# Seven-product pairs for six tiles of the attention branch's projection, in a one-core hybrid layer

## The chip, the core and the metric

The kernel runs on one core of a Trainium2 chip. The metric is the device time of one execution in microseconds (us). The kernel before took 874.84 us, the median of three runs (873.97 to 877.55). The profile shows one further execution.

## The reference, cut to what matters

One layer works on 640 token columns (128 of a prompt, 512 of a sample) and 1024 channels. It has two branches, a gated long convolution ("hyena", `y_h`) and an attention (`y_a`). What the change touches is the end, where both are merged:

```python
mod = silu(cond) @ w_ada + b_ada            # shift, scale, gate
p_h = (y_h * silu(g_h)) @ w_bh
p_a = (y_a * silu(g_a)) @ w_ba
m_h, m_a = split(sigmoid(m), 2, axis=-1)
out = (m_h * p_h + m_a * p_a) @ w_out
x_new = layer_norm(ALPHA * x + gate * out)
```

All tensors are float32.

## The kernel before

**Numbers.** A float32 operand is split into a high part (float32r, made by ScalarE, "ACT") and a low part (the rest, a subtraction on VectorE, "DVE"); see `split`, L100 to L102. A product takes three TensorE ("PE") matmuls: high x high, high x low, low x high. Channels lie on the partitions, tokens along the free axis. A row of 640 tokens is worked on in two halves of 320 columns, one PSUM bank each. All weights are 128 x 1024 tiles of one array `wall`; tiles 80 to 87 (`T_BH`) are `w_bh`, 88 to 95 (`T_BA`) `w_ba`, 96 on (`T_WO`) `w_out`.

**Plain tiles.** `proj` (L175) makes one output tile of 128 channels: 8 blocks of the contraction x 3 passes x 2 halves = 48 matmuls of 320 columns, at L170. Its weight comes through `wraw` (L133, a load into a ring of two raw tiles) and `wtile` (split into a "wh" ring of two and a "wl" ring of three).

**Pairs.** The projections of attention already go another way. `pair_tile` (L1174) makes two output tiles together: with contraction and outputs halved it is a 2 x 2 block product, which it forms from seven products instead of eight (the Winograd form of Strassen's method). The weights' side is prepared by `prepare` (L1142): four sums (L1154) of 512-column blocks, seven operands "wb", each split. The input's side, four sums `t1` to `t4` of the rows and their splits, is made once by `first_sums` and what follows it. A product is 4 blocks x 3 passes = 12 matmuls of 320 columns, at L1189; a pair is 84. Results are put together by ACT and DVE (L1196, L1198, L1204) and handed to a function `use`. After the fourth product the next pair of the list `follow` is prepared.

**Stages.** After the convolution come attention with its projections (from about 388 us; 19 pairs, woven with scores, softmax and values), then the merge in two halves, then the output projection with the norm (L1454, L1469 to L1480). The merge:

- the hyena half: eight plain tiles of `w_bh` on `yhH`, `yhL`. The first two are interleaved by half. Weight `T_BH + 2` is split into a place of its own (L1390). The result is multiplied by the gate row `mh` (L574), a row of the attention branch is loaded and split into `yaH`, `yaL` (L1396 to L1398), and a step of the generator `gate_rows` (L1338) is taken;
- the attention half: eight plain tiles of `w_ba` on `yaH`, `yaL`, multiplied by the gate row `ma`, added to `mh` on DVE (L1427), split into `mH`, `mL`;
- `gate_rows` forms the residual's gate on all partitions: eight loads of 512 KB (`wgate`), two DVE operations of 1024 columns for each (L1346, L1348). `gate_bias` (L1404) sums them over the partitions with 12 short matmuls (L1417) and adds the bias, after tile 4 of the attention half;
- `out_weight` loads and splits the eight tiles of `w_out`, four of them during the attention half.

**Order.** PE's order is the program's in most of the kernel. DVE's and ACT's orders are chosen by the scheduler from data that should be ready, except in instructions that are pinned. In the merge, loads (all issued on SP's queue, L63) keep the program's order; a load whose place isn't free yet holds those behind it. GpSimd ("POOL") carries the softmax's scaling (L1010), and issues the accumulating weight loads of the convolution (L150). The output's constants and residual rows (`bc`, `res`, L1482 to L1487) are loaded once the merge's tiles are released.

Of the kernel before, what the change touches and what calls it, by code (L numbers as in the profile page):

```python
# [9 lines left out]
F32 = mybir.dt.float32  # L10
# [35 lines left out]
def tile_hyena_natten_step(ctx: ExitStack, tc: tile.TileContext, a, o):  # L46
# [211 lines left out]
    def prologue():  # L258
# [19 lines left out]
        def begin(i):  # L278
            if i == 1:
                parts[i] = [[row(yhp, "yh", f"w1{t}{c}", dt)[:, :512] for c in range(2)] for t, dt in (("r", F32), ("h", F32R), ("l", F32R))]  # L280
            else:
                parts[i] = [
                    [t[:, 512 * c : 512 * c + 512] for c in range(2)] for t in (
                        wp.tile([P, 1024], F32, tag="raw", name=f"raw{i}"), wp.tile([P, 1024], F32R, tag="wh", name=f"wh{i}"),
                        wp.tile([P, 1024], F32R, tag="wl", bufs=3, name=f"wl{i}"),
                    )
                ]
            early[i] = [[parts[i][t][k // 4][:, P * (k % 4) : P * (k % 4) + P] for k in range(NK)] for t in (1, 2)]
# [853 lines left out]
    def prepare(i0, i1, pin):  # L1142
        for i in (i0, i1):
            if i not in raws:
                wraw(i)
                loads[i] = last[0]
        ra, rb = raws.pop(i0), raws.pop(i1)
        a11, a12, a21, a22 = (r[:, 512 * h : 512 * h + 512] for r in (ra, rb) for h in range(2))
        src = {0: a11, 4: a12, 5: a22}
        wb = {}  # L1150

        def wsum(j, x, y, op, dst=None):
            src[j] = dst if dst is not None else row(sp, "s", f"s{j}_{i0}", bufs=2)[:, :512]
            ins = nc.vector.tensor_tensor(src[j], x, y, op=op)  # L1154
# [19 lines left out]
    def pair_tile(i0, i1, use):  # L1174
        def halfrow(tag, bufs, name):
            return sp.tile([P, 384], F32, tag=tag, bufs=bufs, name=f"{name}{i0}")[:, :HALF]

        if i0 not in ready:
            prepare(i0, i1, False)
# [2 lines left out]
        for j in range(7):  # L1182
# [18 lines left out]
            else:  # L1201
                if j != 3:
                    c = halfrow("c", 4, f"c{j}_")
                nc.vector.tensor_tensor(c, dst, c if j == 3 else u, op=ALU.add)  # L1204
# [41 lines left out]
    def mix_(m):  # L1246
# [13 lines left out]
    out["slots_r"] = left.enter_context(tc.tile_pool(name="slots_r", bufs=1))  # L1260

    def yh_home(i):
        if i < 4:
# [5 lines left out]
    def yh_raw(n):  # L1269
# [2 lines left out]
                out["stage"] = slot(0, "v", f"yhraw{n}")  # L1272
            yraw[n] = out["stage"][:, NT * (n % 2) : NT * (n % 2) + NT]
        else:
            yraw[n] = slot(1, ("q", "ql")[n % 2], f"yhraw{n}")[:]
        load_to(yraw[n], yh_d[n])
        if n == 2:
            behind(last[0], loads[mix_(6)[1]])
# [34 lines left out]

    with tc.manual_schedule(engines={mybir.EngineType.PE}):
        values_back(1)
        for j in range(8):
            main, n_main = mains(j)
            if j in (3, 5):
# [8 lines left out]
    for n in range(2, NK):  # L1327
        yh_split(n)
        if n in (3, 4):
            yh_raw(n + 3)  # L1330
    mp = tail.enter_context(tc.tile_pool(name="mp", bufs=1, side="right"))
    lp = left.enter_context(tc.tile_pool(name="lp", bufs=1))
# [3 lines left out]
    gbc = lp.tile([P, 2, D], F32, tag="gbc", name="gbc")  # L1336

    def gate_rows():  # L1338
        for k in range(NK):
            raw = slot(k % 2, "v", f"gate{k}")[:, :D]  # L1340
            load_to(raw, a["wgate"][k])
            yield
            for c in range(2):
                s_ = st[:, k, c : c + 1]
                if k == 0:
                    ins = nc.vector.tensor_scalar_mul(gbc[:, c], raw, s_)  # L1346
                else:
                    ins = nc.vector.scalar_tensor_tensor(gbc[:, c], raw, s_, gbc[:, c], op0=ALU.mult, op1=ALU.add)  # L1348
                tc.keep_in_program_order(ins)

    wo = {}

    def wo_row(t, i, n):
        return lp.tile([P, D], F32R, tag=f"{t}{i}", name=f"{t}{i}_{n}")[:]

    def out_weight(k):
        raw = wp.tile([P, D], F32, tag="raw", name=f"wo{k}")
        load_to(raw[:], a["wall"][T_WO + k])
        if k < 4:
            wh, wl = (wo_row(t, k, T_WO + k) for t in ("woh", "wol"))  # L1360
        else:
            if k < 6:
                wh = slot(k - 4, "v", f"woh{k}", F32R)[:, :D]
            else:
                wh = wp.tile([P, D], F32R, tag="wh", name=f"woh{k}")[:]
            if k == 5:
                wl = wp.tile([P, D], F32R, tag="raw", name="wol5")[:]
# [5 lines left out]
    def mixed(src, n, tag, bufs):  # L1373
        th = row(mp, tag, f"{tag}{n}", bufs=bufs)
        load_to(th[:], src[n])
        return th

    side = gate_rows()
    mhs = []
# [6 lines left out]
    for n in range(NK):  # L1386
        if n < 2:
            ps = firsts[n]
        else:
            ps = now(proj(T_BH + n, yhH, yhL, dst=[[wo_row(t, 0, T_BH + n)] for t in ("woh", "wol")] if n == 2 else None))  # L1390
        wraw(T_BH + n + 2)
        th = mixed(mh_d, n, "mh", NK)
        mhs.append(th)
        for p, cs in zip(ps, CS):
            gate(th[:, cs], p)
        raw = slot(1, ("q", "ql")[n % 2], f"yaraw{n}")  # L1396
        load_to(raw[:], ya_d[n])
        split(yaH[n], yaL[n], raw[:])  # L1398
        next(side, None)
    mH, mL = yhH, yhL  # L1400
    eps = lp.tile([P, 1], F32, tag="eps", name="eps")
    nc.gpsimd.memset(eps[:], LN_EPS)

    def gate_bias():  # L1404
        quarter = lp.tile([P, 1], F32R, tag="quarter", name="quarter")
        nc.scalar.activation(quarter[:], eps[:], AF.Copy, scale=0.0, bias=0.25)
        b0 = wp.tile([P, D], F32, tag="raw", name="b0")
        load_to(b0[:], a["rows"][0:1].to_broadcast([P, D]))
        for c in range(2):
            for c0, n in ((0, 384), (384, 384), (768, 256)):  # L1410
                cs = slice(c0, c0 + n)
                gt = out["slots_r"].tile([P, 2, 384], F32R, tag="kl" if (c0 // 384 + c) % 2 else "k", name="gt")
                gh, gl = gt[:, 0, :n], gt[:, 1, :n]
                split(gh, gl, gbc[:, c, cs])
                pg = aux(f"gb{c}{c0}")
                for i, g in enumerate((gh, gl)):
                    nc.tensor.matmul(pg[:, :n], quarter[:].to_broadcast([P, P]), g, start=i == 0, stop=i == 1)  # L1417
                nc.vector.scalar_tensor_tensor(gbc[:, c, cs], b0[:, cs], 0.25, pg[:, :n], op0=ALU.mult, op1=ALU.add)

    for n in range(NK):  # L1420
        ps = now(proj(T_BA + n, yaH, yaL))
        if n < NK - 2:
            wraw(T_BA + n + 2)
        th = mixed(ma_d, n, "ma", 3)
        for p, cs in zip(ps, CS):
            gate(th[:, cs], p)
        nc.vector.tensor_tensor(th[:], th[:], mhs[n][:], op=ALU.add)  # L1427
        split(mH[n], mL[n], th[:])
        next(side, None)
        if 0 < n < 5:  # L1430
            out_weight(n - 1)
        if n == 4:
            gate_bias()

    for k in (4, 6, 7, 5):
        out_weight(k)


    tail.close()
# [190 lines left out]
```

## Time and profile before

| | |
|---|---|
| median of three runs | 874.84 us |
| the profiled execution | 874.77 us |
| its span | 873.0 us |
| TensorE matmul, busy | 861.0 us, 99% |
| VectorE, busy | 645.6 us, 74% |
| ScalarE, busy | 447.1 us, 51% |
| GpSimd, busy | 130.0 us, 15% |
| granted TensorE clock, mean | 0.997 |

The profile has a page (busy shares, 40 slices, the chain of work that ended last, the costliest groups) and views that are asked for: busy time by stage, groups of instructions, the chain and the instructions in order of time, waits. PEld is the loading of the matmuls' weights, which overlaps PE. A row of the timeline gives start, length, engine, line, operation, output <- inputs, shapes, how many; in brackets the idle time before it and who ended it. A row of a group gives the busy time of all, the mean length of one in ns, and the idle time ahead of them. Records on an engine overlap a little at their ends, so an engine's rate is read from the distance of starts.

### The profile page before, as it was taken

How to read it: one execution, taken by the hardware profiler on the slowest of the kernel's cores; microseconds unless marked ns; L12 is line 12 of the kernel's file. 1: busy time of each engine (PE TensorE's matmuls, PEld its weight loads, DVE VectorE, ACT ScalarE, POOL GpSimd, SP SyncE). 2: the span in 40 equal slices, each digit the busy share in tenths (PEclk: the TensorE clock that was granted, in tenths of full speed). 3: DMA queues.
4: the chain of work that ended last, by engine and by line, in shares of the span. 5: the costliest groups of instructions: out<-in, count | busy, mean ns of one | idle time of the engine just before them, and what ended most of it. 6: DMA issues, size and time to landing. Idle time of an engine off the chain costs nothing.

```text
span 873.0 us, 16814 instructions
## 1 busy us (share of the span) xinstructions
PE 861.0 (99%) x6446; PEld 833.0 (95%) x6446; DVE 645.6 (74%) x1310; ACT 447.1 (51%) x952; POOL 130.0 (15%) x143
## 2 busy tenths in 40 slices
PE   8999999999999999999999999999999999999996
PEld 7799999999999999999999999999999999999885
DVE  5685587769559747888977887877878567676656
ACT  4485655545553553646664666655656532233200
POOL 0211010101001010106221243222223100000000
PEclk9999999999999999999999999999999999999998
DMA  8977565566556567764162533533352588545511
GB/s 312 411 180 158 128 140 129 134 142 143 124 136 146 115 177 161 189 182 169 59 190 70 170 115 133 166 113 127 100 173 80 153 296 268 176 160 182 215 68 53
DMA packets 58308, 138.39 MB, mean 159 GB/s; under 512 B 8655, under 2 KB 25171, under 8 KB 58228
## 3 DMA queue, kind: packets, MB, share of 16 engines
q1 hardware_dynamic: 47140, 111.69, 38.5%
q0 software_dynamic: 5472, 19.93, 14.0%
q10 hardware_dynamic: 5616, 5.70, 1.9%
q8 instruction: 51, 0.84, 0.4%
q14 instruction: 29, 0.24, 0.1%
HBM read 121.17 MB, written 16.12 MB: 157 GB/s over the span
## 4 chain that ended last, share of the span: by engine, by line
PE 95%; DMA 2%; ACT 2%; DVE 1%; issue 0%; POOL 0%; DVEq 0%; ACTq 0%; POOLq 0%
PE mm L170 36%; PE sp L1189 27%; PE out L1454 6%; PE v L926 5%; PE pt L1028 3%; PE s L1035 3%; PE s L988 2%; PE mm L184 2%; DMA ada<-wada 2%; PE ve L938 1%; DMA wl<-wall 1%; PE adaT L253 1%; PE adaT L270 1%; PE yb L159 1%; PE yb L158 1%; PE yb L160 1%
## 5 line engine op out<-in xcount | busy, mean ns | idle before, releaser
L1189 PE MATMUL sp<-t,wb 128*128 128x320 f32 x912 | 142.0, 310 | 0.0
L1189 PEld LDWEIGHTS sp<-t,wb 128*128 128x128 f32 x912 | 135.2, 188 | 0.9 <-issue 0.7
L170 PE MATMUL mm<-hH,wh 128*128 128x320 f32 x480 | 112.8, 313 | 0.3 <-ACT hH L370 0.3
L170 PE MATMUL mm<-hL,wh 128*128 128x320 f32 x480 | 112.7, 310 | 0.0
L170 PE MATMUL mm<-hH,wl 128*128 128x320 f32 x480 | 112.6, 310 | 0.1
L1189 PE MATMUL sp<-hH,wb 128*128 128x320 f32 x456 | 111.2, 314 | 0.0
L170 PEld LDWEIGHTS mm<-hH,wh 128*128 128x128 f32 x480 | 80.1, 188 | 2.5 <-issue 1.4
L170 PEld LDWEIGHTS mm<-hL,wh 128*128 128x128 f32 x480 | 80.8, 188 | 0.9 <-DVE hL L378 0.4
L170 PEld LDWEIGHTS mm<-hH,wl 128*128 128x128 f32 x480 | 80.8, 188 | 0.8 <-DMA wl<-wall 0.3
L1189 PEld LDWEIGHTS sp<-hH,wb 128*128 128x128 f32 x456 | 78.5, 188 | 2.3 <-issue 2.1
L151 ACT ACTIVATE wh<-raw 128x1024 fp32r<-128x1024 f32 x38 | 40.4, 1062 | 73.4 <-PE mm L170 65.5
L150 POOL DMA_DIRECT2D wl<-wall x38 | 33.0, 868 | 299.5 <-ACT wl L149 238.8
L1189 PE MATMUL sp<-hL,wb 128*128 128x320 f32 x228 | 70.4, 309 | 0.0
L101 ACT ACTIVATE wb<-s 128x512 fp32r<-128x512 f32 x76 | 46.4, 629 | 31.0 <-DVE s L1154 24.2
L1010 POOL TENSOR_SCALAR p<-p,sm 128x384 f32<-128x384 f32 x32 | 44.3, 1393 | 103.7 <-DVE sm L1009 103.7
L102 DVE TENSOR_TENSOR wb<-s,wb 128x512 fp32r<-128x512 f32 x76 | 51.9, 697 | 7.9 <-ACT wb L101 7.7
L101 ACT ACTIVATE wb<-raw 128x512 fp32r<-128x512 f32 x57 | 35.8, 629 | 40.0 <-PE sp L1189 20.8
L102 DVE TENSOR_TENSOR wb<-raw,wb 128x512 fp32r<-128x512 f32 x57 | 40.6, 712 | 8.6 <-ACT wb L101 8.6
L1454 PE MATMUL out<-woh,yhs 128*128 128x512 f32 (+1 forms) x176 | 45.5, 372 | 0.0
L1189 PEld LDWEIGHTS sp<-hL,wb 128*128 128x128 f32 x228 | 42.9, 188 | 0.0
L170 PE MATMUL mm<-yhs,wh 128*128 128x320 f32 x224 | 41.9, 309 | 0.0
L149 ACT ACTIVATE wl<-raw 128x1024 fp32r<-128x1024 f32 x38 | 40.8, 1075 | 0.0
(377 smaller groups left out, 2038.5 us busy)
## 6 DMA issues: line engine op xcount, KB each, us to landing
raw<-wall SPq DMA_DIRECT2D x93, 512.0 KB, 3.7
wl<-wall POOLq DMA_DIRECT2D x38, 512.0 KB, 5.8
ada<-wada SPq DMA_DIRECT2D x16, 512.0 KB, 5.6
tm<-bias SPq DMA_DIRECT2D x16, 512.0 KB, 4.4
gate<-wgate SPq DMA_DIRECT2D x8, 512.0 KB, 4.3
wo<-wall SPq DMA_DIRECT2D x8, 512.0 KB, 4.1
xt<-xT SPq DMA_DIRECT2D x8, 320.0 KB, 7.3
dec<-decay SPq DMA_DIRECT2D x20, 128.0 KB, 3.3
```

The costliest lines, as they stand in the source:

```text
L101: hi = nc.scalar.activation(dst_h, src, AF.Copy)
L102: return hi, (eng or nc.vector).tensor_tensor(dst_l, src, f(dst_h), op=ALU.subtract)
L149: nc.scalar.activation(wl, raw[:], AF.Copy, scale=-1.0)
L150: nc.gpsimd.dma_start(wl, a["wall"][i], accum_op=ALU.add)
L151: nc.scalar.activation(wh, raw[:], AF.Copy)
L170: nc.tensor.matmul(ps[hf][:, :HALF], wt[k], x[:, hf * HALF : (hf + 1) * HALF], start=(i == 0 and k == 0), stop=(i == lead[2] and k == NK - ...
L926: nc.tensor.matmul(ps[t // 2][:, t % 2 * 256 : t % 2 * 256 + 256], x[:, k, P * t : P * t + P], wk, start=first and t % 2 == 0, stop=last, ...
L1010: nc.gpsimd.tensor_scalar_mul(pv, pv, sm[:, 2:3])
L1028: nc.tensor.transpose(pt[:, i * P : i * P + P], x, ident)
L1035: nc.tensor.matmul(dst, lhs, rhs, start=start, stop=stop, skip_group_check=True)
L1189: nc.tensor.matmul(dst, wk, x(xi, k), start=j < 4 and k == 0 and i == 0, stop=k == 3 and i == 2, skip_group_check=True,)
L1454: ins = nc.tensor.matmul(dst, m[k][:, c0 : c0 + P], w[:, c : c + n], start=(first and k == 0), stop=(last and k == 5), skip_group_check=True,)
```

## The change

- Tiles 0 to 5 of the attention half go through `pair_tile` as three pairs; tiles 6 and 7 stay plain.
- The four sums of the attention branch's rows are made in the hyena half (`turned_sums`), as rows land; rows are loaded in the order 0, 4, 1, 5, 2, 6, 3, 7.
- The addition of both branches moves from DVE to POOL, by half-rows, and trails a pair behind (`finish`).
- The gate rows move into attention: one DVE operation behind the fourth product of 16 of the 19 pairs, with one raw tile for the loads. `gate_bias` moves behind the first output tile, with 8 matmuls of 512 columns, and its bias row is loaded behind the residual rows.
- Weights of the hyena half are split two tiles ahead, and the third one loses its own place.
- The raw weight ring has three tiles; the rings `s` and `c` of the pairs are cut to size.
- The descriptor ring of DMAs issued by POOL shrinks from its default to 2048 bytes a partition, which frees SBUF.

```diff
-        raws[i] = wp.tile([P, 1024], F32, tag="raw", name=f"raw{i}")
+        raws[i] = wp.tile([P, 1024], F32, tag="raw", bufs=3, name=f"raw{i}")
...
+            if j == 3 and i0 in GATED_AT:
+                gate_row(after)
+                gate_load()
             if j == 3 and (i0, i1) in follow:
                 prepare(*follow[i0, i1], True)
...
+    GATED_AT = [runs[0][i][0] for i in (0, 1, 2, 3, 5, 6, 7, 8, 10, 11, 12, 13, 15, 16, 17, 18)]
...
+    def gate_row(after):
+        k, c = divmod(gate_n[0], 2)
+        s_ = st[:, k, c : c + 1]
+        if k == 0:
+            ins = nc.vector.tensor_scalar_mul(gbc[:, c], gate_raw[k], s_)
+        else:
+            ins = nc.vector.scalar_tensor_tensor(gbc[:, c], gate_raw[k], s_, gbc[:, c], op0=ALU.mult, op1=ALU.add)
+        behind(ins, after)
+        tc.keep_in_program_order(ins)
+        gate_n[0] += 1
...
+    def turned_sums(k):
+        b11, b12 = (ya_raw[k][:, cs] for cs in CS)
+        b21, b22 = (ya_raw[k + 4][:, cs] for cs in CS)
+        prev = {}
+        for t, x, y, op in (
+            ("t1", b12, b11, ALU.subtract), ("t3", b22, b12, ALU.subtract),
+            ("t2", "t1", b22, ALU.subtract), ("t4", "t2", b21, ALU.add),
+        ):
+            d = prev[t] = sp.tile([P, HALF], F32, tag="c", bufs=4, name=f"y{t}_{k}")[:]
+            nc.vector.tensor_tensor(d, prev.get(x) if type(x) is str else x, y, op=op)
+            split(ts[t][0][:, k], ts[t][1][:, k], d)
...
+        for n in range(NK):
+            ps = firsts[n] if n < 2 else now(proj(T_BH + n, yhH, yhL))
+            wraw(T_BH + n + 2)
...
+            load_to(mh(n), mh_d[n])
+            for p, cs in zip(ps, CS):
+                gate(mh(n)[:, cs], p)
+            if n < NK - 2:
+                early[T_BH + n + 2] = wtile(T_BH + n + 2)
+            ya_row(YA[n])
...
+        def merged(n, hf, src):
+            th = mas[n][:, CS[hf]]
+            gate(th, src)
+            pending.append((n, hf, th))
...
+        def finish():
+            if not pending:
+                return
+            n, hf, th = pending.pop(0)
+            nc.gpsimd.tensor_tensor(th, th, mh(n)[:, CS[hf]], op=ALU.add)
+            split(mH[n][:, CS[hf]], mL[n][:, CS[hf]], th)
...
+        for p, (i0, i1) in enumerate(pairs):
+            for i in (1, 0):
+                ma(2 * p + i)
+            for i, _ in enumerate(pair_tile(i0, i1, lambda i, hf, src: merged(2 * p + i, hf, src), ya_operand)):
+                if i in (1, 3, 5, 7):
+                    finish()
+                if p == 2 and i == 4:
+                    wraw(T_BA + 6)
+                    wraw(T_BA + 7)
+        for n in (6, 7):
+            ps = now(proj(T_BA + n, yaH, yaL))
+            ma(n)
+            for hf in range(2):
+                merged(n, hf, ps[hf][:, :HALF])
+            while pending:
+                finish()
+            for k in (0, 1) if n == 6 else (2, 3):
+                out_weight(k)
+        for k in (4, 6, 7, 5):
+            out_weight(k)
...
         ps = out_tile(t, ((0, 512), (512, 256), (768, 256)) if t == 4 else ())
+        if t == 0:
+            gate_bias()
         norm_tile(t, ps, t == 4)
...
-    nc = _bacc.Bacc("TRN2", target_bir_lowering=False, num_devices=1)
+    nc = _bacc.Bacc("TRN2", target_bir_lowering=False, num_devices=1, dynamic_dma_scratch_size=2048)
```

More of the change, by code (lines that the diff above doesn't have):

```diff
@@ L1203, in pair_tile @@
                     c = halfrow("c", 4, f"c{j}_")
-                nc.vector.tensor_tensor(c, dst, c if j == 3 else u, op=ALU.add)
+                after = nc.vector.tensor_tensor(c, dst, c if j == 3 else u, op=ALU.add)
                 if j != 2:
@@ L1315, in tile_hyena_natten_step @@
         values_back(1)
+        before = last[0]
+        gate_load()
+        behind(last[0], before)
         for j in range(8):
@@ L1366, in out_weight @@
             if k == 5:
[L1367 removed]
+                wl = wp.tile([P, D], F32R, tag="raw", bufs=3, name="wol5")[:]
             else:
@@ L1385, in tile_hyena_natten_step @@
         firsts = [now(gen) for gen in firsts]
[L1386 to L1436, printed above, removed]
+        for n in range(NK):
+            ps = firsts[n] if n < 2 else now(proj(T_BH + n, yhH, yhL))
+            wraw(T_BH + n + 2)
+            if n % 2 == 0:
+                mhp.append(mp.tile([P, 2 * NT], F32, tag=f"mh{n}", name=f"mh{n}"))
+            load_to(mh(n), mh_d[n])
[4 more added lines that the diff above has]
+            ya_row(YA[n])
@@ new lines, in gate_bias @@
+        def gate_bias():
+            quarter = lp.tile([P, 1], F32R, tag="quarter", name="quarter")
+            nc.scalar.activation(quarter[:], eps[:], AF.Copy, scale=0.0, bias=0.25)
+            b0 = gp.tile([P, D], F32, tag="gr", name="b0")
+            load_to(b0[:], a["rows"][0:1].to_broadcast([P, D]))
+            for c in range(2):
+                for half in range(2):
+                    cs = slice(512 * half, 512 * half + 512)
+                    g2 = fin.tile([P, D], F32R, tag="r", bufs=2, name="gt")
+                    gh, gl = g2[:, :512], g2[:, 512:]
+                    split(gh, gl, gbc[:, c, cs])
+                    pg = aux(f"gb{c}{half}")
+                    for i, g in enumerate((gh, gl)):
+                        nc.tensor.matmul(pg[:], quarter[:].to_broadcast([P, P]), g, start=i == 0, stop=i == 1)
+                    nc.vector.scalar_tensor_tensor(gbc[:, c, cs], b0[:, cs], 0.25, pg[:], op0=ALU.mult, op1=ALU.add)
@@ new lines, in tile_hyena_natten_step @@
+        pairs = [(T_BA + 2 * p, T_BA + 2 * p + 1) for p in range(3)]
+        for x, y in zip(pairs, pairs[1:]):
+            follow[x] = y
+        for p, (i0, i1) in enumerate(pairs):
[7 more added lines that the diff above has]
+                    wraw(T_BA + 7)
```

82 lines of the change are left out of this document (51 added, 31 removed).

## The prediction, made before the result was known

> **What bounds the kernel now.** I read the page first (busy shares, slices, chain), then busy time by stage, then the chain in order of time.
>
> ```profile
> span 873.0 us, 16814 instructions
> PE 861.0 (99%) x6446; PEld 833.0 (95%) x6446; DVE 645.6 (74%) x1310; ACT 447.1 (51%) x952; POOL 130.0 (15%) x143
> ...
> PEclk9999999999999999999999999999999999999998
> ...
> PE 95%; DMA 2%; ACT 2%; DVE 1%; issue 0%; POOL 0%; DVEq 0%; ACTq 0%; POOLq 0%
> ```
>
> TensorE is busy for 99% of the span at full clock and is 95% of the chain that ended last. A busy row need not be a dense one, so the second view takes stages: attention (four rows), the hyena half of the merge, its attention half.
>
> ```profile
> 388.00:436.00 48.00, 48.00 (x367) 46.35 (x367) 43.41 (x119) 32.92 (x92) 19.68 (x16) 1.00 0.37 120
> 436.00:532.00 96.00, 96.00 (x771) 93.27 (x770) 76.80 (x207) 59.01 (x152) 26.16 (x24) 1.00 0.43 139
> 532.00:612.00 80.00, 80.00 (x641) 77.64 (x639) 63.60 (x172) 48.70 (x127) 22.03 (x20) 1.00 0.40 129
> 612.00:695.00 83.00, 83.00 (x693) 79.92 (x692) 63.38 (x165) 52.25 (x129) 23.09 (x21) 1.00 0.41 124
> 695.00:752.00 57.00, 57.00 (x391) 57.00 (x390) 41.38 (x51) 17.80 (x23) 0.00 (x0) 1.00 0.81 275
> 752.00:810.00 58.00, 58.00 (x395) 57.92 (x395) 39.08 (x55) 20.14 (x26) 0.00 (x0) 1.00 0.46 158
> ```
>
> The columns are PE, PEld, DVE, ACT, POOL, then clock and DMA. PE fills every stage. In the merge DVE works 41.38 of 57 us and 39.08 of 58, and POOL nothing. The chain's longest pieces give the price of a matmul:
>
> ```profile
> 406.11 12.32 PE sp L1189 x84
> ...
> 695.21 91.52 PE mm L170 x624
> ...
> 809.70 55.39 PE out L1454 x264
> ```
>
> 91.52 us over 624 matmuls is 146.7 ns for each 320 columns, and 12.32 over 84 is 146.7 as well: a seven-product pair's matmuls run as densely as plain ones, once their operands are there. The merge ends at 809.70, when the output projection starts. The kernel is bound by the number of matmul columns; everything else has to stay out of their way.
>
> **The change, part by part.** *Products.* Six tiles of 48 matmuls (288) become three pairs of 7 x 12 = 84 (252). 36 x 146.7 ns = 5.28 us go from the only path that counts. This is the whole gain; the rest is cost, hidden or not.
>
> *Weights and results of the pairs*, on DVE. The timeline of DVE in attention has operations of both sizes, first with POOL at rest, then (the last two) with POOL at work:
>
> ```profile
> 469.09 0.68 DVE L102 TENSOR_TENSOR wb<-raw,wb 128x512 fp32r<-128x512 f32 x1
> 469.69 0.68 DVE L102 TENSOR_TENSOR wb<-s,wb 128x512 fp32r<-128x512 f32 x1
> 470.30 0.48 DVE L866 SCALAR_TENSOR_TENSOR ql<-c,q 128x320 fp32r<-128x320 f32 x1
> ...
> 498.26 0.48 DVE L574 SCALAR_TENSOR_TENSOR sg<-sg,c 128x320 f32<-128x320 f32 x1
> 498.66 0.68 DVE L1154 TENSOR_TENSOR s<-raw 128x512 f32<-128x512 f32 x1
> ...
> 504.06 0.83 DVE L102 TENSOR_TENSOR wb<-raw,wb 128x512 fp32r<-128x512 f32 x1 [0.35 <-ACT wb L101]
> ...
> 506.09 0.97 DVE L102 TENSOR_TENSOR wb<-s,wb 128x512 fp32r<-128x512 f32 x1
> ```
>
> Starts follow each other after 0.60 us for 512 columns (469.09 to 469.69) and after 0.40 for 320 (498.26 to 498.66). A pair issues 4 weight sums and 7 low parts of 512 columns, and of 320: 5 combinations of products, 4 gates and 4 low parts of the merged half-rows. That is 11 x 0.60 + 13 x 0.40 = 11.8 us of DVE in 84 x 146.7 ns = 12.3 us of PE. It fits, at 96%, where attention runs at about 80%. What makes it hold: five of the seven weights of the first pair are prepared in the hyena half; the last pair prepares none after it; a pair's weights are begun after product 4 of the pair before, so three products (3 x 12 x 146.7 ns = 5.3 us) lie between; and the low parts of merged rows may lag, since only the output projection reads them. I take 0 here, and keep 0 to 3 us of stall for the range. ACT stands at 20.14 of 58 us and has room.
>
> *Sums of the attention branch* (turned sums): 4 sets of 4 sums and 4 low parts of 320 columns, 32 x 0.40 = 12.8 us of DVE in the hyena half, with five weights and two sums of the first pair (about 5 us). The gate rows leave this place:
>
> ```profile
> L1348 DVE SCALAR_TENSOR_TENSOR gbc<-gate,st,gbc 128x1024 f32<-128x1024 f32 x14 | 17.3, 1278 | 0.0
> ...
> L1417 PE MATMUL gb<-gt,quarter 128*128 128x384 f32 (+1 forms) x12 | 3.3, 318 | 0.0
> ```
>
> Most of their 17.3 us was in the 57 us of that row, so DVE stays near 41 to 43 of 57. Cost 0 on the path, as long as the last set of sums comes ahead of the first pair. The gate rows' 8 loads of 512 KB leave the one stage whose DMA share is 0.81, which helps the rows of the attention branch to land.
>
> *Third weight of the hyena half.* It loses its own place, so its split waits until the first tile's matmuls are done. PE does 12 half-steps of 6 matmuls first: 695.21 + 72 x 0.1467 = 705.8, and needs it after 24 more, at 709.3.
>
> ```profile
> 696.79 1.22 DVE L102 TENSOR_TENSOR wol<-raw,woh 128x1024 fp32r<-128x1024 f32 x1
> ...
> 705.66 0.89 DVE L574 SCALAR_TENSOR_TENSOR mh<-mh,mm 128x320 f32<-128x320 f32 x2 [2.65 <-PE mm L170]
> 706.47 0.82 DVE L102 TENSOR_TENSOR ya_hL<-yaraw,ya_hH 128x640 fp32r<-128x640 f32 x1
> ```
>
> Now the split is over at 698.0; then its high part on ACT and 1.22 us on DVE fall between 705.8 and about 708.1, with the gates and one row's split (705.66 to 707.3) as company. About 1 us is spare. I take 0, bounds 0 to 2.
>
> *Gate rows in attention.* 14 x 1.28 us and two shorter ones, about 19 us of DVE, into stages with 4.6 + 19.2 + 16.4 + 19.6 = 59.8 us of DVE idle (the first four window rows). Behind each row on DVE stand the next pair's sums; PE needs them three products later.
>
> ```profile
> DVE c L1204 <- PE sp L1189: 27.9, 32, 2.4
> ...
> DVE s L1154 <- DMA raw<-wall: 5.7, 5, 2.4
> ```
>
> DVE is ahead there: its longest total wait, 27.9 us, is for PE. Only 388 to 436 is tight (90%), with three rows (3.8 us) for 4.6 us of idle time. SP gets 8 loads more, each queued behind a row on DVE through the single raw tile, and the weights are queued behind them. The third raw tile lets one weight load go ahead of that and can shorten the 5.7 us that DVE waits for them; off the path, 0. I take 0 for the move, bounds 0 to 4.
>
> *Addition on GpSimd.* The merge's sum of both branches goes from DVE to POOL, 12 + 4 half-rows of 320 columns.
>
> ```profile
> L304 POOL TENSOR_TENSOR wl<-raw,wh 128x512 fp32r<-128x512 f32 x1 | 1.4, 1383 | 8.3 <-DMA xt<-xT 8.3
> ...
> L304 POOL TENSOR_TENSOR w1l<-w1r,w1h 128x256 fp32r<-128x256 f32 x1 | 1.0, 976 | 0.0
> ```
>
> Between 0.98 (256) and 1.38 us (512), so about 1.1 each, 4.4 us of POOL in a pair. POOL is not idle company for DVE, though:
>
> ```profile
> 503.82 2.14 POOL L1010 TENSOR_SCALAR edge<-edge,sm 128x320 f32<-128x320 f32 x2
> 505.94 2.46 POOL L1010 TENSOR_SCALAR p<-p,sm 128x384 f32<-128x384 f32 x2
> ```
>
> Beside these the low parts at 504.06 and 506.09 take 0.83 and 0.97 us, against 0.68 alone: up to 0.3 us for each POOL instruction, 1.2 us for a pair, which would bring DVE to 13.0 of 12.3 us. Over three pairs that is 2 us of lag, less than the 5.3 us of lead. The Trainium skill ("SBUF — State Buffer", section "Who interferes with whom") says more: a VectorE instruction with two SBUF inputs and a GpSimd one that reads SBUF exclude each other for the whole instruction. By that rule, the direction agrees with the trace and the size of the loss (0.3 us, not a whole 1.1) does not.
>
> *Gate bias* moves behind the first output tile: 8 matmuls of 512 columns for 12 that hold the same 4096 columns, 0. Its row of the bias is now loaded last.
>
> ```profile
> 816.34 0.80 SPq L63 DMA_DIRECT2D bc<-rows  x2
> 817.19 2.69 SPq L63 DMA_DIRECT2D res<-xB  x5
> ```
>
> ```profile
> res<-xB SPq DMA_DIRECT2D x5, 512.0 KB, 8.2
> ```
>
> The first starts 6.6 us after the output projection; the last of these seven is issued at about 819.5 and lands 8.2 us later, near 828, so one costs about (828 - 816.3) / 7 = 1.7 us. The bias would land at about 829.4, 19.7 us after the projection's start, and two operations of 0.60 on DVE and the first multiplication follow: 21.5. The first tile's result must leave PSUM before the third tile, 22 us (two fifths of 55.39) after the start. I take 0, bounds 0 to 2.
>
> *Smaller ring.* Only the weights on POOL's queue use it:
>
> ```profile
> wl<-wall POOLq DMA_DIRECT2D x38, 512.0 KB, 5.8
> ```
>
> 38 transfers, all before attention (388 us), are one in about 9 us and land after 5.8: rarely two under way. 0.
>
> *Sum:* profiled execution 874.77 us (1.8 outside its span of 873.0, unchanged) - 5.28 = 869.5; from the median of 874.84, **869.6 us**, 0.6% faster. About 0.5% (4.4 us) is what a measurement of this kernel can tell from no change.
>
> **Rivals.** (1) *DVE becomes the bound of the pairs* or one of the tight places above costs something: 1 to 5 us of the gain are lost, 870.5 to 874.8. For: 96% of DVE, POOL beside it, 1 us of spare time at the third weight. Against: the lead of 5.3 us, and the dense 84 matmuls at 406.11 in a stage with DVE at 90%. (2) *The last sums come late.* If DVE keeps the order of the program, the last turned sums stand behind the gates of the last hyena tile, which wait for PE. Then after its last matmul come 2 gates, a row's split, 8 operations, 2 weight sums and the first low part: 0.8 + 0.7 + 3.2 + 1.2 + 0.6 = 6.5 us, with ACT between them some 7.5 of idle PE: 877.1, slower than before. It decides from 5.3 us of stall on. Against: before, DVE's order leaves the program's wherever data are ready (the split at 696.79 runs ahead of the gates at 705.66). (3) *Attention stalls.* Each of 16 gate rows holds sums and, through SP, weights. At 0.33 us of PE stall a row the gain is gone, at 0.6 (9.7 us) it is 879.3; at the full 1.28 us, 890. Against: 59.8 us of idle DVE. (4) *POOL locks DVE for the whole of each add*: 4.4 us more in a pair, 16.2 for 12.3; three pairs 11.7 us, less the lead, 6.4: 876. The rule of the skill named above would give this; the rows show 0.3 us.
>
> **How the numbers follow.** Forecast (869 to 870.4) 0.52; rival 1 0.22; rival 2 0.09; rival 4 0.03; rival 3 beyond 879.2 0.11, and 0.03 for a gain beyond the sum through earlier weights. The range takes the forecast and rivals 1, 2 and 4: 868.6 to 877.1. Faster by over 0.5% (below 870.5) 0.55, within 0.34, slower 0.11.
>
> **What would show it.** The chain should have one PE piece of about 37.0 us for 252 L1189 matmuls behind the hyena half, and the output projection should start about 5.3 us earlier. A gap of PE ahead of the first pair speaks for rival 2, gaps at each pair with DVE above 95% for rivals 1 and 4, gaps between 388 and 695 for rival 3. A late first multiplication by the gate with PE idle 22 us into the output projection would show the bias load. I am wrong if the merge isn't shorter by 5 us or attention isn't as long as now.

## The result: 0.4% faster, with the profile after

The changed kernel takes 872.04 us (median of 20 runs, 870.94 to 876.2), the kernel before 874.86 (20 runs, 873.97 to 879.83). The ratio is 0.9962, with an interval of 0.9947 to 0.9976: 3.3 us less (2.1 to 4.6; the medians differ by 2.8), where 5.28 were forecast. That is within 0.5% of no change, and the first rival's time rather than the forecast's. The profiled execution took 872.68 us.

The page of the changed kernel, in the lines that answer to those of before:

```profile
span 870.7 us, 16878 instructions
...
PE 856.9 (98%) x6406; PEld 827.5 (95%) x6406; DVE 674.8 (78%) x1380; ACT 461.8 (53%) x992; POOL 154.1 (18%) x159
...
PEclk9999999999999999999999999999999999999999
...
PE 90%; DVE 3%; DMA 3%; ACT 1%; issue 0%; SPq 0%; POOL 0%; DVEq 0%; POOLq 0%
```

TensorE issues 40 matmuls fewer (36 of the pairs, 4 of the gate bias, whose 4096 columns are the same), still at full clock. But its share of the chain that ended last has gone from 95% to 90%. Part of that lies in the first 60 us, where the chain now runs over loads (more on this below and in the last section); DVE, from 1% to 3%, has come in near the end. So there are now places where PE waits. The chain in order of time shows where (start, length, what):

```profile
696.27 56.32 PE mm L170 x384
752.59 7.05 PE sp L1190 x48
...
776.67 2.20 DVE s L1155 x2
...
787.54 3.78 PE sp L1190 x24
791.32 14.08 PE mm L170 x96
805.40 11.09 PE out L1521 x48
```

The hyena half is dense: 384 matmuls in 56.32 us are 146.7 ns each. So are the two plain tiles (96 in 14.08). Between them lie the three pairs, from 752.59 to 791.32: 38.73 us for 252 matmuls, where 252 x 146.7 ns would be 36.97. They lose 1.76 us, and the chain leaves PE there for DVE (the weight sums, L1155, among other work). The view of busy time by stage has the same (PE, PEld, DVE, ACT, POOL, then clock and DMA):

```profile
696.00:752.50 56.50, 56.50 (x387) 56.50 (x387) 40.94 (x74) 24.07 (x41) 0.10 (x1) 1.00 0.58 200
...
764.00:791.00 27.00, 26.19 (x174) 25.27 (x173) 26.97 (x48) 13.07 (x25) 8.55 (x9) 1.00 0.35 108
```

In the hyena half DVE has 15.6 us to spare. From 764 on, through the second and third pair, it is busy for 26.97 of 27.00 us: it has become the bound there. PE's own stops in this stretch (idle time ahead of an instruction in square brackets, with what ended it) are for DVE:

```profile
773.93 2.03 PE L1190 MATMUL sp<-ya_t,wb 128*128 128x320 f32 x12 [0.21 <-DVE c L1205]
780.33 5.40 PE L1190 MATMUL sp<-ya_t,wb 128*128 128x320 f32 x34 [0.55 <-DVE wb L102]
```

The records overlap, so the brackets show less than is lost: by the distance of starts these two stops cost 0.48 and 0.82 us, and two shorter ones, at 782.2 and 787.5, cost 0.14 and 0.31, 1.75 in all.

Attention isn't longer. Its first matmuls and the first of the hyena half stand in the chains of the two kernels, of before and then of after:

```profile
388.53 0.88 PE sp L1189 x6
```

```profile
389.59 0.88 PE sp L1190 x6
```

With 695.21 (before) and 696.27 (after) that is 306.68 us in both. The 1.06 us by which the changed kernel comes later are lost long before: 16 matmuls that wait for two early loads (`ada`, L253) start at 27.92 before and at 28.96 after, and this start of the kernel differs between executions that run the same program there (last section). So the stretch from the start of the hyena half to the end of the span is compared below: 873.0 - 695.2 = 177.8 us before and 870.7 - 696.3 = 174.4 after, 3.4 us less, close to the measured 3.3 and to 5.28 - 1.76 = 3.5.

### The profile page after: what moved, and what is told of

Read it like the earlier page. It is cut to its first block, busy times and chain, and to the rows that moved or that the text cites. A ratio compares the mean times of both kernels' runs of the same rounds, so it can differ in the third digit from the quotient of the medians.

```text
span 870.7 us, 16878 instructions
## 1 busy us (share of the span) xinstructions
PE 856.9 (98%) x6406; PEld 827.5 (95%) x6406; DVE 674.8 (78%) x1380; ACT 461.8 (53%) x992; POOL 154.1 (18%) x159
## 4 chain that ended last, share of the span: by engine, by line
PE 90%; DVE 3%; DMA 3%; ACT 1%; issue 0%; SPq 0%; POOL 0%; DVEq 0%; POOLq 0%
PE mm L170 30%; PE sp L1190 29%; PE out L1521 6%; PE v L926 5%; PE pt L1028 3%; PE s L1035 3%; PE s L988 2%; DMA ada<-wada 2%; PE mm L184 2%; PE ve L938 1%; DMA dec<-decay 1%; DVE wb L102 1%; DMA wl<-wall 1%; DVE s L1155 1%; PE adaT L270 1%; PE yb L159 1%
## 5 line engine op out<-in xcount | busy, mean ns | idle before, releaser
L101 ACT ACTIVATE wb<-s 128x512 fp32r<-128x512 f32 x88 | 53.8, 628 | 40.4 <-DVE s L1155 26.1
L102 DVE TENSOR_TENSOR wb<-s,wb 128x512 fp32r<-128x512 f32 x88 | 60.3, 699 | 8.0 <-ACT wb L101 8.0
L101 ACT ACTIVATE wb<-raw 128x512 fp32r<-128x512 f32 x66 | 41.3, 627 | 45.2 <-PE sp L1190 21.5
L102 DVE TENSOR_TENSOR wb<-raw,wb 128x512 fp32r<-128x512 f32 x66 | 47.1, 713 | 5.0 <-ACT wb L101 4.8
L170 PE MATMUL mm<-yhs,wh 128*128 128x320 f32 x256 | 48.0, 309 | 0.0
L1010 POOL TENSOR_SCALAR edge<-edge,sm 128x320 f32<-128x320 f32 x32 | 42.2, 1330 | 0.5 <-DVE sm L1009 0.5
L1205 DVE TENSOR_TENSOR c<-sp,u 128x320 f32<-128x320 f32 x66 | 31.9, 483 | 12.5 <-PE sp L1190 12.5
```

The source lines that it names most:

```text
L101: hi = nc.scalar.activation(dst_h, src, AF.Copy)
L102: return hi, (eng or nc.vector).tensor_tensor(dst_l, src, f(dst_h), op=ALU.subtract)
L170: nc.tensor.matmul(ps[hf][:, :HALF], wt[k], x[:, hf * HALF : (hf + 1) * HALF], start=(i == 0 and k == 0), stop=(i == lead[2] and k == NK - ...
L1010: nc.gpsimd.tensor_scalar_mul(pv, pv, sm[:, 2:3])
L1205: after = nc.vector.tensor_tensor(c, dst, c if j == 3 else u, op=ALU.add)
```

## Where 1.76 us of the gain went

DVE's work in the pairs was forecast at 96% of PE's time, plus at most 0.3 us for each instruction of POOL beside it. The timelines of POOL and of DVE in the changed kernel, the same stretch, show what an addition on POOL does (start, length):

```profile
760.82 1.19 POOL L1462 TENSOR_TENSOR ma<-ma,mh 128x320 f32<-128x320 f32 x1 [60.49 <-DVE ma L574]
763.04 1.26 POOL L1462 TENSOR_TENSOR ma<-ma,mh 128x320 f32<-128x320 f32 x1 [1.03 <-DVE ma L574]
767.34 0.88 POOL L1462 TENSOR_TENSOR ma<-ma,mh 128x320 f32<-128x320 f32 x1 [3.04 <-DVE ma L574]
```

```profile
760.60 0.68 DVE L1155 TENSOR_TENSOR s<-raw,raw 128x512 f32<-128x512 f32 x1
761.20 1.36 DVE L102 TENSOR_TENSOR wb<-raw,wb 128x512 fp32r<-128x512 f32 x1
...
763.49 1.36 DVE L1155 TENSOR_TENSOR s<-raw 128x512 f32<-128x512 f32 x1
...
767.18 0.48 DVE L1205 TENSOR_TENSOR c<-sp,u 128x320 f32<-128x320 f32 x1
```

A 512-column operation that takes 0.68 us elsewhere takes 1.36 when it begins inside an addition: the second one begins at 763.49, POOL ends at 763.04 + 1.26 = 764.30, and DVE ends 0.55 later. It goes the other way too: an addition that begins during a DVE operation with both inputs in SBUF takes 1.19 or 1.26 us; the one at 767.34 begins during an operation that has one input in PSUM (`sp`, at 767.18) and takes 0.88. The Trainium skill ("SBUF — State Buffer", section "Who interferes with whom") calls it an exclusive lock on a shared pair of ports; for these additions the trace agrees with it, where the prediction had set it aside.

The rows of before on which the prediction set it aside can be read again. The low part that begins 0.24 us into a POOL instruction (504.06 against 503.82) is 0.15 us longer than alone, and the one that begins 0.15 us into another (506.09 against 505.94) is 0.29 us longer; one that begins 1.00 us into the next (508.16 against 507.16) takes its usual 0.69. So, as an estimate from these rows, each of these instructions of 1.1 to 1.2 us held DVE off only for its first 0.4 us (0.24 + 0.15, 0.15 + 0.29), and what the prediction took for the price was what was left of that. For an addition the same working gives more: the one that ends at 764.30 can have begun its 0.88 us at 763.42, the DVE operation that begins at 763.49 is 0.68 us longer, and 0.07 + 0.68 is 0.75 us of hold.

The theory: each addition stops DVE for most of its time, DVE falls behind with the weights, and PE runs into it in the second and third pair. The rival: DVE's own operations fill the pairs and would do so with POOL at rest; the lengthening falls where nobody waits. The runs x1 to x4 tell these apart, x5 and x6 take the moved parts by themselves, x7 shows how the lag builds up, and x8 to x11 ask what else the change would bear.

## The experiments

**x1: without the addition.**

```diff
-            nc.gpsimd.tensor_tensor(th, th, mh(n)[:, CS[hf]], op=ALU.add)
```

> The changed kernel without the addition of both branches (the hyena half's product is left out of the result), so POOL does nothing in the pairs. In the changed kernel the three pairs take 38.7 us on PE instead of 37.0, with DVE busy 26.97 of 27.0 us. Theory 1 (exclusion): DVE is full because POOL's additions hold up its operations with two SBUF inputs, 5.0 us of lengthening in all; without them the pairs take 37.0 to 37.3 us and the kernel is 1.4 to 1.8 us faster than the changed one. Theory 2 (plain load): 11.8 us of DVE work in a pair of 12.3, with its waits for ACT and PE, is too much by itself; the pairs stay at 38.3 us or more and the gain is under 0.5 us.

869.71 us (6 runs) beside 875.08 before: 0.9943 [0.9923, 0.9963]. In the chain the three pairs are one piece:

```profile
751.24 36.97 PE sp L1190 x252
```

No stop is left, and 36.97 is 252 x 146.7 ns to the hundredth. From the start of the hyena half to the end of the span it takes 867.6 - 694.9 = 172.7 us, 1.7 less than the changed kernel. DVE has all its other work still (11.31 of 12.30 us in the second pair and 11.61 of 12.35 in the third, where 11.8 was forecast), so the rival falls: what overfills the pairs is the addition.

**x2: the addition on DVE.**

```diff
-            nc.gpsimd.tensor_tensor(th, th, mh(n)[:, CS[hf]], op=ALU.add)
+            nc.vector.tensor_tensor(th, th, mh(n)[:, CS[hf]], op=ALU.add)
```

> The additions on DVE instead of POOL: 12 more operations of 0.40 us, 4.8 us, in and behind the pairs, and no lengthening (5.0 us less). Theory 1 (exclusion): the two cancel, pairs of 38.2 to 39.2 us, time within 0.5 us of the changed kernel. Theory 2 (plain load, exclusion unimportant): DVE gets 1.6 us more in each pair that was full already, pairs of 41 us or more, 2.5 to 4 us slower than the changed kernel.

871.86 us (12 runs): 0.9964 [0.9951, 0.9976], the same as with POOL. The stage row of the second and third pair, and PE's one stop in it:

```profile
764.00:791.00 27.00, 25.90 (x176) 25.64 (x176) 26.93 (x56) 11.79 (x22) 0.00 (x0) 1.00 0.43 135
```

```profile
778.74 2.47 PE L1190 MATMUL sp<-ya_t,wb 128*128 128x320 f32 x15 [1.10 <-DVE wb L102]
```

DVE is as full as before this edit (26.93 of 27), with 56 instructions for 48 and none lengthened. The pairs take 38.34 us, within the first theory's range. Giving the addition to POOL took nothing from DVE.

**x3: the addition by a DMA that accumulates.**

```diff
-            nc.gpsimd.tensor_tensor(th, th, mh(n)[:, CS[hf]], op=ALU.add)
+            if n < 6:
+                nc.gpsimd.dma_start(th, mh(n)[:, CS[hf]], accum_op=ALU.add)
+            else:
+                nc.gpsimd.tensor_tensor(th, th, mh(n)[:, CS[hf]], op=ALU.add)
```

> The additions of the three pairs as accumulating DMAs from POOL's queue (160 KB each); the last two tiles keep POOL's additions. Theory 1: POOL no longer reads SBUF beside DVE, the pairs take 37.0 to 37.4 us and the kernel is 1.2 to 1.8 us faster than the changed one. Against it: writing the descriptors might hold DVE as an addition does, or the transfers might land so late that the gate rows' places aren't free; then pairs of 38.3 us or more.

870.02 us (6 runs): 0.9939 [0.9924, 0.9955]. Chain, stage row and one issue on POOL:

```profile
750.95 36.97 PE sp L1190 x252
```

```profile
764.00:791.00 27.00, 27.00 (x187) 27.00 (x186) 23.36 (x46) 11.82 (x22) 7.45 (x9) 1.00 0.71 181
```

```profile
763.61 0.86 POOL L1463 DMA_DIRECT2D ma<-mh  x1 [1.73 <-DVE ma L574]
```

The whole sum is computed and the pairs are dense; from the start of the hyena half it takes 867.5 - 694.6 = 172.9 us, 1.5 less than the changed kernel. POOL's busy time here is the issuing, and DVE has 3.6 us to spare again. DVE's groups of operations over the pairs give the price (count | busy us, mean ns | idle time ahead), first of the changed kernel, then of x3:

```profile
L102 DVE TENSOR_TENSOR wb<-s,wb 128x512 fp32r<-128x512 f32 x10 | 7.5, 760 | 0.2 <-ACT wb L101 0.2
L102 DVE TENSOR_TENSOR wb<-raw,wb 128x512 fp32r<-128x512 f32 x8 | 6.1, 768 | 0.8 <-ACT wb L101 0.8
L102 DVE TENSOR_TENSOR yhs<-ma,yhs 128x320 fp32r<-128x320 f32 x8 | 5.0, 628 | 0.0
...
L102 DVE TENSOR_TENSOR wl<-raw,wh 128x1024 fp32r<-128x1024 f32 x2 | 3.1, 1554 | 0.0
L1155 DVE TENSOR_TENSOR s<-raw 128x512 f32<-128x512 f32 x2 | 2.7, 1373 | 0.0
L1155 DVE TENSOR_TENSOR s<-s,raw 128x512 f32<-128x512 f32 x2 | 1.7, 826 | 0.0
```

```profile
L102 DVE TENSOR_TENSOR wb<-s,wb 128x512 fp32r<-128x512 f32 x10 | 6.8, 684 | 0.2 <-ACT wb L101 0.2
L102 DVE TENSOR_TENSOR wb<-raw,wb 128x512 fp32r<-128x512 f32 x8 | 5.4, 685 | 0.8 <-ACT wb L101 0.8
L102 DVE TENSOR_TENSOR yhs<-ma,yhs 128x320 fp32r<-128x320 f32 x8 | 3.9, 487 | 1.7 <-ACT yhs L101 1.7
...
L102 DVE TENSOR_TENSOR wl<-raw,wh 128x1024 fp32r<-128x1024 f32 x2 | 2.4, 1221 | 0.1
...
L1155 DVE TENSOR_TENSOR s<-raw 128x512 f32<-128x512 f32 x2 | 1.4, 686 | 0.0
L1155 DVE TENSOR_TENSOR s<-s,raw 128x512 f32<-128x512 f32 x2 | 1.4, 686 | 0.0
```

The same operations in the same counts cost 0.7 + 0.7 + 1.1 + 0.7 + 1.3 + 0.3 = 4.8 us more beside ten additions on POOL: 0.5 us for each, which is what an addition costs on DVE itself (0.48 for 320 columns).

**x4: the additions of the first two pairs only in the last part of the third.**

```diff
-                if i in (1, 3, 5, 7):
+                if p == 2 and i in (7, 9, 11, 13):
                     finish()
```

The rows of tiles 4 and 5 are then put into a free slot, since the earlier ones are held longer.

> The additions and splits of the first two pairs are put off until the last weights of the third pair are begun (its product 4), with tiles 4 and 5 of the gate rows in another place; POOL still adds. Both theories: DVE loses up to 8 low parts and the lengthening from the time that the pairs are prepared in; pairs of 37.0 to 37.4 us. Rival: the work put off collides with the output weights' splits, and the output projection starts as late as in the changed kernel or stalls in its first tile; then the pairs are short and the whole time is unchanged within 0.5 us.

872.07 us (9 runs): 0.9963 [0.995, 0.9977], and neither expectation was met. PE stops in the same places. The POOL timeline says why: the additions start at 760.26, 762.48 and 766.78, each 0.56 us ahead of the changed kernel's, as the whole merge does. Their place in the program was changed, and their order on the engine was not. So this run tells nothing of an addition that really comes later; that stays open.

**x5: the moves without the pairs.** The kernel before with the gate rows in attention (`GATED_AT`, `gate_row`), three raw weight tiles and the small ring:

```diff
-        raws[i] = wp.tile([P, 1024], F32, tag="raw", name=f"raw{i}")
+        raws[i] = wp.tile([P, 1024], F32, tag="raw", bufs=3, name=f"raw{i}")
...
+            if j == 3 and i0 in GATED_AT:
+                gate_row(after)
+                gate_load()
...
-    nc = _bacc.Bacc("TRN2", target_bir_lowering=False, num_devices=1)
+    nc = _bacc.Bacc("TRN2", target_bir_lowering=False, num_devices=1, dynamic_dma_scratch_size=2048)
```

> The kernel before with the gate rows in attention, three raw tiles and the small ring, and no pairs in the merge. If the move is free (as the prediction took it), attention lasts 306.7 us on PE as before and the time stays within 0.5 us of the kernel before, or a little below where the merge's loads have more room. Rival: the move itself costs, and the missing 2 us of the change are partly here; then attention is longer by 1 us or more and the kernel is slower than before.

874.97 us (12 runs) beside 874.83: 0.9994 [0.9982, 1.0005]. Its chain has attention's first and the hyena half's first piece at

```profile
388.75 0.88 PE sp L1189 x6
...
695.44 4.11 PE mm L170 x28
```

306.69 us apart. Sixteen more operations on DVE, eight loads, the ring and the third tile cost nothing that can be measured.

**x6: the gate rows back in the hyena half** of the changed kernel, two behind each tile:

```diff
-            if j == 3 and i0 in GATED_AT:
-                gate_row(after)
-                gate_load()
...
+            gate_load()
+            for _ in range(2):
+                gate_row(None)
```

> The changed kernel with the gate rows back in the hyena half (all eight, pinned). DVE works 40.9 of 56.5 us there in the changed kernel; 18.8 us more is over the stage. If DVE bounds this end of the kernel, the first pair's sums come late or the pairs stall more: 2 to 8 us slower than the changed kernel. If the 15.6 us of idle time take them, no more than 0.5 us slower.

881.45 us (6 runs): 1.0082 [1.0054, 1.011], 9.4 us behind the changed kernel and slower than before. Stage rows, and PE's stops ahead of and in the first pair:

```profile
695.00:752.50 57.50, 57.50 (x393) 57.31 (x392) 48.67 (x74) 21.98 (x34) 0.10 (x1) 1.00 0.66 234
752.50:800.00 47.50, 40.13 (x246) 38.52 (x245) 46.38 (x79) 20.30 (x38) 10.71 (x10) 0.89 0.43 142
```

```profile
757.57 0.90 PE L1190 MATMUL sp<-ya_t,wb 128*128 128x320 f32 x2 [4.58 <-ACT wb L101]
760.05 7.78 PE L1190 MATMUL sp<-ya_t,wb 128*128 128x320 f32 x34 [1.58 <-DVE wb L102]
```

DVE goes into the pairs with work left over, is busy for 46.38 of 47.50 us, and PE stands 4.58 and 1.58 us for the first weights. The sums come late, as in the prediction's second rival, but not for its reason alone: DVE's timeline has it waiting 1.49 us for a gate row's load (at 750.90), and the last row of `mh` lands only at about 754.5, so how much is DVE's work and how much the eight loads' was not separated. The granted clock has a part as well: 34 matmuls from 760.05 to 767.66 take 7.61 us instead of 4.99, at a clock of 0.63. So of the 9.6 us by which the first pair is longer than in the changed kernel (21.9 for 12.3), 6.2 are these two stops and 2.6 the slower matmuls.

**x7: two pairs instead of three.**

```diff
-        pairs = [(T_BA + 2 * p, T_BA + 2 * p + 1) for p in range(3)]
+        pairs = [(T_BA + 2 * p, T_BA + 2 * p + 1) for p in range(2)]
```

> The changed kernel with two pairs and four plain tiles (POOL still adds). 12 matmuls more, 1.76 us. If the stalls build up from pair to pair because DVE can't keep up (0.0, 0.5 and 1.3 us over 12.2 in the three pairs of the changed kernel), the third pair won only about 0.5 us: within 0.7 us of the changed kernel. If they come from something at the start of the stage, 1.5 us or more slower.

871.99 us (12 runs): 0.997 [0.9955, 0.9985]. Chain:

```profile
752.18 7.05 PE sp L1190 x48
...
777.30 28.16 PE mm L170 x192
```

Two pairs take 777.30 - 752.18 = 25.12 us for 168 matmuls (dense: 24.65), so they lose 0.47 of the 1.76 us. The lag builds up: the third pair saves 1.76 us of products and loses 1.29 again.

**x8: four pairs, additions by DMA.** With `range(4)` and x3's edit; the last pair's addition is on DVE.

> All eight tiles as four pairs, additions of the first three by DMA as in the run with DMA additions, of the last by DVE. 12 matmuls fewer than that run: 1.76 us faster than it, if the output weights' splits, which have no plain tiles to hide beside, keep ahead of the first output tile (1.38 us of PE for each of eight weights, 1.13 us of DVE). Otherwise the first output tile stalls: as much time as that run, or 1 to 4 us slower.

871.1 us (6 runs): 0.9949 [0.9931, 0.9966], no better than x3. The first three pairs are dense and the fourth loses 0.2 us; the first output tile, where a stall was feared, is dense too. What is new comes later in the output projection, whose first matmul stands at 799.0, ahead of the last product, and the others from 801.0 on. From DVE's timeline:

```profile
824.51 1.88 DVE L1482 SCALAR_TENSOR_TENSOR gbc<-b,gb 128x512 f32<-128x512 f32 x3 [4.60 <-DMA b<-rows]
```

The bias row lands 25.5 us after that first matmul (23.5 after the second), and the third output tile stands 2.2 us (2.4 from start to start, with one matmul in it). In the changed kernel the same load is hidden, as forecast (DVE's timeline there):

```profile
823.91 1.88 DVE L1479 SCALAR_TENSOR_TENSOR gbc<-b,gb 128x512 f32<-128x512 f32 x3 [4.96 <-DMA b<-rows]
```

18.5 us after 805.40, where 19.7 was forecast and 22 is the limit. The load keeps its place while the merge shortens, and so comes onto the path.

**x9: as x8, with the bias row loaded ahead of the pairs.**

```diff
+        b0 = gp.tile([P, D], F32, tag="gr", name="b0")
+        load_to(b0[:], a["rows"][0:1].to_broadcast([P, D]))
+        pairs = [(T_BA + 2 * p, T_BA + 2 * p + 1) for p in range(4)]
```

> The run with four pairs, with the row of the bias loaded ahead of the pairs instead of behind the residual rows. That run started the output projection earlier than the one with three pairs and DMA additions but stood 2.4 us ahead of the third output tile, because the bias landed 25.5 us after the projection's start. If that load is all that held it, the gap goes and the kernel is 2.4 us faster than that run, about 868.7 us. Rival: the norm's other inputs (residual rows, loaded after the last weights) hold the third tile as well; then at most 1 us is won.

869.95 us (9 runs) beside 875.03: 0.9946 [0.9927, 0.9965]. That is 1.2 us faster than x8, by the medians and from the start of the hyena half on, where 2.4 was expected if the load was all. One stop of 1.1 us (1.3 from start to start) is left in the output projection, with another name on DVE's side of it than the rival's residual rows:

```profile
824.90 0.69 DVE L1480 SCALAR_TENSOR_TENSOR gbc<-b,gb 128x512 f32<-128x512 f32 x1 [4.18 <-PE gb L1479]
```

Now it is the last matmul of the gate bias, late in PE's own order.

**x10: as x9, with the gate bias in the hyena half**, behind tiles 4 and 5.

```diff
+            if n == 3:
+                load_to(b0[:], a["rows"][0:1].to_broadcast([P, D]))
+            if n in (4, 5):
+                gate_bias(n - 4)
```

> Four pairs with DMA additions, and the whole gate bias (its splits, its 8 matmuls, its row) in the hyena half, where DVE has over 10 us of idle time. In the run with the early bias row the third output tile still stood 1.3 us, now behind the last matmuls of the gate bias, which stand late in PE's order. If that was what was left, PE has no gap in the output projection and from the first values' matmul to the end it takes 563.8 us instead of 565.1 (872 us of the changed kernel: 567.2). Rival: the gate bias delays the hyena half's sums and the first pair stalls by as much.

873.3 us (12 runs): 0.997 [0.9954, 0.9986], worse, and not as I expected. The output projection is dense, but PE stands in the hyena half:

```profile
733.48 0.50 PE L1422 MATMUL gb<-gt,quarter 128*128 128x512 f32 x1 [1.59 <-DVE gt L102]
```

That is one stop of two like it; by the whole trace PE stands 4.2 us in this half. One call needs four tiles of a ring of three, so its second part waits for the matmuls of its first, and PE waits for that with the hyena half behind it. The first pair is dense, so the rival didn't happen either.

**x11: as x10, in four parts**, one behind each of the tiles 2 to 5.

```diff
+            if n == 1:
+                load_to(b0[:], a["rows"][0:1].to_broadcast([P, D]))
+            if 2 <= n < 6:
+                gate_bias((n - 2) // 2, n % 2)
```

> As the run before it (four pairs, DMA additions, gate bias in the hyena half), with the gate bias in four parts behind four different tiles. There the output projection had no gap left, but PE stood 4.2 us in the hyena half for the fourth split of each half of the bias, whose place comes free only behind the first part's matmuls. With one part to a tile that wait has 7 us of other matmuls to hide behind: no gap, 564.1 us from the first values' matmul to the end, 868.5 to 869.5 us in all, the fastest here. Rival: the pinned loads behind the bias row hold the attention branch's rows, and the first pair stalls.

868.56 us (7 runs) beside 875.02: 0.9916 [0.9896, 0.9935], the fastest of all, 7.3 us ahead of the kernel before by the ratio (0.0084 x 875.02), 6.5 by the medians. Chain, with the first piece of the hyena half:

```profile
699.94 21.12 PE mm L170 x144
...
758.10 47.54 PE sp L1190 x324
...
807.63 55.40 PE out L1519 x263
```

Four pairs without a stop that shows, and a dense output projection. From the start of the hyena half to the end of the span it takes 871.0 - 699.9 = 171.1 us, against 174.4 in the changed kernel and 177.8 before.

## Why the prediction was right in direction and short in size

- **The bound and the products: right.** 36 x 146.7 ns = 5.28 us is there in full as soon as nothing stands in the way (x1 and x3: 36.97 us for 252 matmuls).
- **Turned sums, third weight, gate rows in attention, ring, third raw tile: right at 0.** The hyena half is dense at 56.32 us, attention takes 306.68 us in both kernels, and x5 measures the moved parts alone at 0.9994. The move wasn't idle, though: x6 shows 9.4 us without it. Late sums, the second rival, show only there, where the gate rows stay; the third rival didn't happen.
- **Gate bias: right at 0**, with the bias at 18.5 us for a forecast of 19.7. That the price was hidden and not absent is seen in x8.
- **Addition on GpSimd: the step that failed.** "Up to 0.3 us for each POOL instruction, 1.2 us for a pair", "2 us of lag, less than the 5.3 us of lead". The rows behind 0.3 were of POOL instructions with one input; these additions have two, and the runs show up to 0.7 us on one DVE operation, 4.8 us over ten additions, 0.5 us for each. That brings DVE from 11.8 to about 11.8 + 4 x 0.5 = 13.8 us for a pair of 12.3. By the stage rows DVE is busy for 9.54 of 12.30 us in the first pair, for 12.80 of 12.80 in the second and for 13.57 of 13.60 in the third. Whether it is the second input that makes the hold longer was not measured by itself.
- **The lead failed with it.** Three products ahead is room in the order of the program. To use it, DVE would have to be done with the pair before, and it is idle only where it can't work ahead, as its timeline at the end of the changed kernel's hyena half shows:

```profile
752.48 0.88 DVE L574 SCALAR_TENSOR_TENSOR mh<-mh,mm 128x320 f32<-128x320 f32 x2 [4.75 <-PE mm L170]
```

Those 4.75 us are lost: ACT, which makes the next weight's high part, stands behind the same matmuls (5.90 us, until 752.39). In the first pair DVE is idle for another 2.8 us, for ACT and PE. After that it doesn't get ahead again. This account of the lead is read from the timeline; no run tests it. The loss is 1.76 us: the first rival's size (0 to 3 us of stall were kept for the pairs), by the fourth rival's mechanism, which I had given the whole 1.1 us an addition and a chance of 0.03.
- **The marker for the end of the merge was off.** I said that the output projection would start 5.3 us earlier. It starts at 805.40 for 809.70, 4.3 earlier, though the merge lost 1.76 us and the start was 1.06 late: the gate bias's matmuls have left the merge. Four of them are a piece of 0.92 us in the chain,

```profile
816.49 0.92 PE gb L1478 x4
```

so the eight are 1.84, and 5.28 - 1.76 + 1.84 - 1.06 = 4.3. They come back behind it, and the gain is 3.5 and no more. The prediction's last sign, a merge that isn't shorter by 5 us, failed for the same reason: the merge is shorter by 5.36 us (114.49 to 109.13), of which 1.84 only moved. The signs that did speak were the missing piece of 37.0 us and PE's stops in the pairs with DVE full.

## What to carry to other kernels

Here an addition of two operands in SBUF, given to GpSimd, was not taken off VectorE: it cost VectorE as much as the addition itself (0.5 us for 0.48). Where VectorE is nearly full (92 to 94% in x1, without the additions), count it there as well, and try an accumulating DMA if the data may lag. Where matmuls are saved, set each helper's work in the shorter time, and take a lead only where the helper is free to build it. A load or a small step that is hidden by a few microseconds keeps its place when the stage ahead of it shrinks, so each further gain of that size asks again what is late next.

## What the runs showed of the hardware

- VectorE and GpSimd, both with two inputs in SBUF, held each other up in both directions: 0.68 us became 1.36 on the one, 0.88 became 1.19 to 1.66 on the other. Accumulating DMAs from SBUF to SBUF, issued by POOL in 0.86 us, left VectorE's 512-column operations at 684 ns.
- The start of the kernel differs between executions. The first 60 us of before and of x11 (a stage row of each):

```profile
0.00:60.00 60.00, 56.01 (x545) 49.18 (x546) 37.12 (x75) 35.83 (x75) 7.60 (x22) 1.00 0.87 305
```

```profile
0.00:60.00 60.00, 53.63 (x514) 46.76 (x515) 32.32 (x68) 31.05 (x66) 6.73 (x21) 0.94 0.87 306
```

The DMA engines are busy for 87% of it in both, and PE has done 545 and 514 matmuls when the 60 us are over. The program is not quite the same there, since x11 has the third raw tile and the small ring; but the changed kernel and x1 to x4, which run the same program as x11 in this stretch, had done 538 and 541 to 548. In x11's the granted clock was 0.94 there. Where the edit lies behind it, comparing stretches of two traces from a common instruction takes this out; comparing spans doesn't.
